# Gate and up projections as seven block products in place of eight, in a hand-ordered loop

## The chip, the cores and the metric

One core of a Trainium2 chip runs the whole layer in one launch. The metric is the device time in microseconds of that launch: 829.66 us is the median of 3 runs of the kernel before.

## What is computed

One decoder layer on 512 tokens with 1024 features: a mixer (dilated attention beside retention), a cross-attention to 256 memory rows, and a SwiGLU of 2816 hidden features, each between an RMSNorm of its input and an RMSNorm of its output, and added to the residual. The part that the change touches:

```python
def swiglu(h, w_gate_up, w_down):
    g, u = jnp.split(h @ w_gate_up, 2, axis=-1)
    return (jax.nn.silu(g) * u) @ w_down

for l in range(DEPTH):
    y = hybrid_mixer(rms_norm(x, pre_mix_g[l]), ...)
    x = x + rms_norm(y, post_mix_g[l])
    y = memory_cross_attn(rms_norm(x, pre_mem_g[l]), ...)
    x = x + rms_norm(y, post_mem_g[l])
    y = swiglu(rms_norm(x, pre_ffn_g[l]), w_gate_up[l], w_down[l])
    x = x + rms_norm(y, post_ffn_g[l])
```

## The kernel before, in words

The chip's engines are told of by their names in the trace: PE multiplies matrices, PEld loads its weights, DVE, ACT and POOL work element by element, SP issues most transfers. All data are fp32. Each factor of a product is kept as a high half (rounded to fp32r) and a low half (the rest), and `mm3` makes each product of three matmuls, high x high (L84), high x low (L85), low x high (L86). `split` makes the halves: ACT casts (L90), DVE subtracts (L91), so a weight block of 128x2048 costs ACT two casts and DVE two subtractions 1024 wide.

Weights come as transfers of 1 MB in a fixed order (`chunks`). `load` puts one into `raw` (two buffers) and splits it; `take` keeps one or two blocks ahead. So a fetch starts when the low half of the block two before it has freed the buffer.

The four blocks of 128 tokens end the memory attention one after another (`mem_block`, L780): 48 matmuls of the output projection, then `residual` (squares on ACT, the small per-token arithmetic of the reciprocal root on POOL, L137 to L141 and L625, the sums on DVE) and `normed` (the same again, then `h`, one DVE instruction 128x1024, L635). PE transposes `h` (L792) and `split` stores it feature by feature in `h3` (`to_h3`, L787). PE's order there: transposes of block 0, projection of block 2, transposes of block 1, projection of block 3, gate/up column block 0 for the first 256 tokens, transposes of block 2, column block 1 for the first 256 tokens, transposes of block 3, then both for the other 256.

The 22 column blocks of the gate/up product hold 128 gate and 128 up features each. From the third on (L834 to L838) one takes 2 x 8 x 3 = 48 matmuls of 512 columns (all tokens), gate into one PSUM bank and up into another; ACT takes the silu of the gate (L817), DVE multiplies by up (L820). `split_a` (L841) splits the result for the down projection, its low half on POOL (L846). The order of instructions on each engine is set by the framework's scheduler from the order of the code; the buffers decide what waits.

Of the kernel before, what the change touches and what calls it, by code (L numbers as in the profile page):

```python
# [11 lines left out]
F32 = mybir.dt.float32  # L12
# [7 lines left out]
P = 128  # L20
D = 1024
# [17 lines left out]
def hybrid_layer(ctx, tc, t, out):  # L39
# [20 lines left out]
    def pair(name):  # L60
        return unit(name + "h", F32R), unit(name + "l", F32R)
# [17 lines left out]
    def part(pr, c0, n):  # L79
        return pr[0][:, c0:c0 + n], pr[1][:, c0:c0 + n]  # L80
# [7 lines left out]
    def split(src, hi, lo, scale=None):  # L88
# [75 lines left out]

    def load_gain(name):
        g = wk.tile([P, D], F32, tag="g", name=uname("g"), bufs=2)
        src = t[name]
        nc.sync.dma_start(g, bass.AP(tensor=src.tensor, offset=src.offset, ap=[[0, P], [1, D]]))
        return g

# [7 lines left out]

# [1 line left out]
    gT = cp.tile([P, 3, KT], F32, name="gT")  # L180
# [70 lines left out]

# [1 line left out]
    def tok_proj(c0, name, evict):  # L253
# [48 lines left out]

# [1 line left out]
    off = [0, 512, 1024, 896]  # L304
# [62 lines left out]

# [1 line left out]
    qk = [unit("qk", F32R) for _ in range(4)]  # L369
# [50 lines left out]

# [1 line left out]
    scale = AD ** -0.5  # L422
# [86 lines left out]

# [1 line left out]
    mem = {}  # L511
# [74 lines left out]
    for i in range(AH):  # L586
# [12 lines left out]
        att_values(i)  # L599
# [176 lines left out]
    nat = tuple(range(KT))  # L776
    g4 = load_gain("pre_ffn_g")
    h3 = [pair("h3") for _ in range(2)]
# [26 lines left out]
    af = []  # L805

    def gx(k, c0, n):
        return part(h3[k // 4], (k % 4) * S + c0, n)

    def gate_up(w, pg, pu, c0, n):  # L810
        for j, ps in enumerate((pg, pu)):
            for k in range(KT):
                mm3(ps[:, c0:c0 + n], part(w, k * 256 + j * P, P), gx(k, c0, n), k == 0, k == KT - 1)

    def swish(f, pg, pu):
        sg = work("sg")
        nc.scalar.activation(sg, pg, AF.Silu)  # L817
# [93 lines left out]
def _layout(inp):  # L911
# [62 lines left out]
```

## Time and profile before

| What | Value |
|---|---|
| median of 3 runs | 829.66 us (829.64 to 830.22) |
| span of the profiled execution (the only time given of it) | 828.5 us |
| PE busy | 807.9 us, 98% |
| DVE busy | 396.6 us, 48% |
| ACT busy | 305.4 us, 37% |
| POOL busy | 132.8 us, 16% |

Busy times are sums of the intervals in which an engine worked on something; an engine with a low share can still be what another waits for at one place. The span stands in the same place as a run's time, without the little that lies around it.

### The profile page before, as it was taken

The page shows a single profiled execution, that of the slowest core. Times are in us where ns is not written, and L with a number is a line of the kernel's source. Part 1 is how long each engine was busy: PE and PEld are TensorE (multiplying, and loading weights), DVE is VectorE, ACT ScalarE, POOL GpSimd, SP SyncE. Part 2 cuts the span into 40 slices and gives each one's busy share as a digit, 9 for nine tenths or more (in the row PEclk, how much of TensorE's full clock was granted, in tenths as well). Part 3 has the DMA queues.
Part 4 walks back from the last instruction along what each step waited for, and adds up shares of the span by engine and source line. Part 5 has one row for each costly group of instructions (what it writes and reads, how often), then busy time and mean ns, then how long its engine had stood idle before and what let it go on. Part 6 is the DMA issues. An engine that isn't in the chain of part 4 may idle for free. (4 is left out here: it accounts for less than half of the span.)

```text
span 828.5 us, 10220 instructions
## 1 busy us (share of the span) xinstructions
PE 807.9 (98%) x4108; PEld 675.7 (82%) x4108; DVE 396.6 (48%) x766; ACT 305.4 (37%) x537; POOL 132.8 (16%) x176
## 2 busy tenths in 40 slices
PE   9979999999999999999999899999999999999996
PEld 7768888877777878999988788888888888888884
DVE  5595168764565657758446441405050314222144
ACT  5504333466464733445435232222130305332110
POOL 0161024410110100300036300000000004236000
PEclk9998999999999999999999999999999999999998
DMA  8726212221124440524002340505050322521011
GB/s 305 291 77 236 94 51 87 73 95 52 51 70 175 163 153 0 197 109 153 1 1 102 127 153 1 203 1 203 1 203 1 121 82 74 182 102 51 1 51 51
DMA packets 15519, 85.86 MB, mean 104 GB/s; under 512 B 1904, under 2 KB 1904, under 8 KB 6896
## 3 DMA queue, kind: packets, MB, share of 16 engines
q1 hardware_dynamic: 14752, 84.16, 27.7%
q10 hardware_dynamic: 720, 1.06, 0.3%
q8 instruction: 32, 0.52, 0.3%
q14 instruction: 15, 0.12, 0.0%
HBM read 83.11 MB, written 2.10 MB: 103 GB/s over the span
## 5 line engine op out<-in xcount | busy, mean ns | idle before, releaser
L91 DVE TENSOR_TENSOR wl<-raw,wh 128x1024 fp32r<-128x1024 f32 (+1 forms) x135 | 166.5, 1267 | 102.6 <-ACT wh L90 70.2
L90 ACT CAST wh<-raw 128x1024 fp32r<-128x1024 f32 (+1 forms) x135 | 133.8, 1042 | 95.3 <-DMA raw<-in_w_in 38.1
L820 DVE TENSOR_TENSOR af<-sg,u 128x512 f32<-128x512 f32 x22 | 15.1, 686 | 133.7 <-PE u L86 133.7
L846 POOL TENSOR_TENSOR al<-af,ah 128x512 fp32r<-128x512 f32 x22 | 34.6, 1605 | 257.5 <-ACT ah L845 243.3
L84 PE MATMUL g<-h3h,wh 128*128 128x512 f32 (+1 forms) x192 | 72.1, 375 | 0.0
L84 PE MATMUL u<-h3h,wh 128*128 128x512 f32 (+1 forms) x192 | 71.7, 373 | 0.0
L85 PE MATMUL g<-h3l,wh 128*128 128x512 f32 (+1 forms) x192 | 71.3, 371 | 0.0
L86 PE MATMUL g<-h3h,wl 128*128 128x512 f32 (+1 forms) x192 | 71.3, 371 | 0.0
L85 PE MATMUL u<-h3l,wh 128*128 128x512 f32 (+1 forms) x192 | 71.3, 371 | 0.0
L86 PE MATMUL u<-h3h,wl 128*128 128x512 f32 (+1 forms) x192 | 71.3, 371 | 0.0
L84 PE MATMUL dn<-wh,ah 128*128 128x512 f32 x176 | 68.5, 389 | 0.0
L85 PE MATMUL dn<-wl,ah 128*128 128x512 f32 x176 | 68.5, 389 | 0.0
L86 PE MATMUL dn<-wh,al 128*128 128x512 f32 x176 | 68.5, 389 | 0.0
L817 ACT ACTIVATE sg<-g 128x512 f32<-128x512 f32 x22 | 13.1, 598 | 149.2 <-PE g L86 123.0
L84 PEld LDWEIGHTS g<-h3h,wh 128*128 128x128 f32 x192 | 36.5, 190 | 6.5 <-ACT h3h L90 0.2
L84 PEld LDWEIGHTS u<-h3h,wh 128*128 128x128 f32 x192 | 36.6, 191 | 6.3
L85 PEld LDWEIGHTS g<-h3l,wh 128*128 128x128 f32 x192 | 36.2, 188 | 6.4
L86 PEld LDWEIGHTS g<-h3h,wl 128*128 128x128 f32 x192 | 36.2, 188 | 6.2
L85 PEld LDWEIGHTS u<-h3l,wh 128*128 128x128 f32 x192 | 36.2, 188 | 6.2
L86 PEld LDWEIGHTS u<-h3h,wl 128*128 128x128 f32 x192 | 36.1, 188 | 6.1
L84 PEld LDWEIGHTS dn<-wh,ah 128*128 128x128 f32 x176 | 33.0, 188 | 6.9
L86 PEld LDWEIGHTS dn<-wh,al 128*128 128x128 f32 x176 | 33.0, 188 | 6.9
(267 smaller groups left out, 1752.8 us busy)
## 6 DMA issues: line engine op xcount, KB each, us to landing
raw<-in_w_gu SPq DMA_DIRECT2D x22, 1024.0 KB, 4.8
raw<-in_w_in SPq DMA_DIRECT2D x12, 1024.0 KB, 5.1
raw<-in_w_dn SPq DMA_DIRECT2D x11, 1024.0 KB, 4.7
raw<-in_w_kv SPq DMA_DIRECT2D x8, 1024.0 KB, 4.7
x<-in_x SPq DMA_DIRECT2D x4, 1024.0 KB, 10.2
raw<-in_w_out SPq DMA_DIRECT2D x4, 1024.0 KB, 5.3
raw<-in_w_q SPq DMA_DIRECT2D x4, 1024.0 KB, 5.3
raw<-in_w_o SPq DMA_DIRECT2D x4, 1024.0 KB, 4.7
```

The source lines that it names most:

```text
L84: nc.tensor.matmul(o, lhsT=sh, rhs=mh, start=start, stop=False)
L85: nc.tensor.matmul(o, lhsT=sh, rhs=ml, start=False, stop=False)
L86: nc.tensor.matmul(o, lhsT=sl, rhs=mh, start=False, stop=stop)
L90: nc.scalar.copy(hi, src)
L91: nc.vector.tensor_sub(lo, src, hi.bitcast(F32))
L817: nc.scalar.activation(sg, pg, AF.Silu)
L820: nc.vector.tensor_mul(af[-1][:, (f % 4) * S:(f % 4 + 1) * S], sg, pu)
L846: nc.gpsimd.tensor_sub(lo[:, c], af[i][:, c], hi[:, c].bitcast(F32))
```

## The change

For the column blocks from the third on, the weights [gate over up] and the features are taken as 2 x 2 blocks (gate and up, first and last 512 features) and the tokens as two halves. In place of eight products of blocks seven are made, with sums of weight blocks (four per column block: s1, s3, s2, s4, on POOL) and sums of activation blocks (T1 to T4, made once), and the products are added to the results after. A product is 4 x 3 matmuls of 256 columns. Column blocks 0 and 1 keep eight products (`plain`).

- `blocks_sum` makes the four sums of 128x512 (L116 to L119) from `raw`; `blocks_split` splits 512 columns of `raw` (only the block that product 4 needs), the other 1024, and the two halves of the sums: 512 + 3 x 1024 in place of 2 x 1024.
- `step(f)` is the loop; `manual_schedule` keeps its order on every engine. Results: ACT copies a product out of PSUM (L879), DVE adds five times 256 columns and once 512, silu is in place on SBUF (L888), the product with up reads SBUF twice (L894).
- The small arithmetic of `mem_block` moves from POOL to DVE; the low halves of column blocks 0 and 1 move from DVE to POOL (L948).
- The tokens' `x` is written to DRAM ahead of the loop and read back behind it, to free room. Gains are loaded by pairs. `wk` has 6 buffers in place of 4.

```diff
-    def mem_block(b, mid=None):
-        residual(out_proj((b,), o_lhs, wo, nat, "o2", 0, mid)[b], b, g3, nc.gpsimd)
-        return normed(b, g4, nc.gpsimd)
+    def mem_block(b, mid=None):
+        e = nc.vector
+        residual(out_proj((b,), o_lhs, wo, nat, "o2", 0, mid)[b], b, g3, e)
+        return normed(b, g4, e)
...
+    def blocks_sum(f):
+        raw = blocks[f][0]
+        a11, a12, a22, a21 = (raw[:, i * 512:(i + 1) * 512] for i in range(4))
+        sums = rawp.tile([P, 2048], F32, tag="sums", name=uname("sums"))
+        s2, s4, s1, s3 = (sums[:, i * 512:(i + 1) * 512] for i in range(4))
+        nc.gpsimd.tensor_add(s1, a21, a22)
+        nc.gpsimd.tensor_sub(s3, a11, a21)
+        nc.gpsimd.tensor_sub(s2, s1, a11)
+        nc.gpsimd.tensor_sub(s4, a12, s2)
+        blocks[f] += [sums, pair("wa"), pair("wb")]
+
+    def blocks_split(f, i):
+        raw, sums, wa, wb = blocks[f]
+        src, w, c0, n = ((raw, wa, 1024, 512), (raw, wa, 0, 1024), (sums, wb, 1024, 1024), (sums, wb, 0, 1024))[i]
+        split(src[:, c0:c0 + n], *part(w, c0, n))
...
+    def to_b(h, b):
...
+        split(pv[0], *bview("B12", c0))
+        split(pv[1], *bview("B22", c0))
+        nc.vector.tensor_sub(t1, pv[0], braw[:, 0, :, c0:c0 + P])
+        nc.scalar.copy(b12, pv[0])
+        nc.vector.tensor_sub(t2, pv[1], t1)
+        nc.vector.tensor_sub(t3, pv[1], b12)
+        nc.gpsimd.tensor_sub(t4, braw[:, 1, :, c0:c0 + P], t2)
+        return lambda: [split(v, *bview(n, c0)) for v, n in ((t2, "T2"), (t1, "T1"), (t4, "T4"), (t3, "T3"))]
...
+    prods = {1: (0, 0, "B11"), 2: (0, 512, "B21"), 4: (0, 1024, "T4"), 5: (1, 1024, "T1"),
+             6: (1, 0, "T2"), 7: (1, 1536, "T3"), 3: (1, 512, "B22")}
+    def product(i, w, ps):
+        u, c0, name = prods[i]
+        for k in range(4):
+            x_ = bx[name][:, k * H:(k + 1) * H], bx[name][:, 1024 + k * H:1024 + (k + 1) * H]
+            mm3(ps, part(w[u], c0 + k * P, P), x_, k == 0, k == 3)
...
+    def ffn_c1(f):
+        nc.scalar.copy(s1[:, :H], p[:, :H])
+    def ffn_c11(f):
+        nc.vector.tensor_add(c[:, :H], s1[:, :H], p[:, H:])
+    def ffn_done(f):
+        nc.vector.tensor_add(c[:, H:], c[:, H:], r[:, H:])
+        nc.scalar.activation(c, c, AF.Silu)
+    def ffn_mult(f):
...
+        nc.vector.tensor_mul(af[-1][:, (f % 4) * S:(f % 4 + 1) * S], c, u)
+    def step(f):
+        nxt = f + 1 < FT
+        ffn_p12(f)
+        w, p, s1, c, u = ffn[f]
+        if f + 2 < FT:
+            blocks_sum(f + 2)
+        if f > PRE:
+            ffn_done(f - 1)
+        if nxt:
+            blocks_split(f + 1, 0)
+        ffn_c1(f)
+        if f > PRE:
+            ffn_mult(f - 1)
+        if nxt:
+            blocks_split(f + 1, 1)
+        if f + 3 < FT:
+            blocks_fetch(f + 3)
+        ffn_c11(f)
+        q, r = bank("q2"), bank("r")
+        ffn[f] += (r,)
+        product(4, w, q[:, :H])
+        product(6, w, r[:, :H])
+        if nxt:
+            blocks_split(f + 1, 2)
+        nc.vector.tensor_add(s1[:, H:], s1[:, :H], r[:, :H])
+        product(5, w, q[:, H:])
+        if nxt:
+            blocks_split(f + 1, 3)
+        nc.vector.tensor_add(c[:, H:], s1[:, H:], q[:, H:])
+        product(7, w, p[:, :H])
+        nc.vector.tensor_add(s1[:, :H], s1[:, H:], p[:, :H])
+        nc.vector.tensor_add(u.rearrange("p (i s) -> p i s", i=2), q.rearrange("p (i s) -> p i s", i=2),
+                             s1[:, None, :H].to_broadcast([P, 2, H]))
+        product(3, w, r[:, H:])
...
+    def plain_load(f):
+        blocks_fetch(f)
+        raw, w = blocks[f][0], pair("wa")
+        for i in range(4):
+            c = slice(i * 512, (i + 1) * 512)
+            nc.scalar.copy(w[0][:, c], raw[:, c])
+            nc.gpsimd.tensor_sub(w[1][:, c], raw[:, c], w[0][:, c].bitcast(F32))
...
-    for f in range(2, FT):
-        w, pg, pu = take("w_gu", f), bank("g"), bank("u")
-        gate_up(w, pg, pu, 0, S)
-        swish(f, pg, pu)
+    xd = tc.dram_tile([S, D], F32, name="xd")
+    for b in range(TB):
+        nc.sync.dma_start(xd[b * P:(b + 1) * P, :], x[b])
+    with tc.manual_schedule():
+        for f in range(PRE, FT):
+            step(f)
+        ffn_done(FT - 1)
+        ffn_mult(FT - 1)
+    bx.clear()
+    x = [unit("x") for _ in range(2)]
+    for i in range(2):
+        nc.sync.dma_start(x[i].rearrange("p (b d) -> p b d", b=2), xd[i * 256:(i + 1) * 256, :].rearrange("(b p) d -> p b d", p=P))
```

**DVE in the loop.** The rows of the kernel before from the last blocks, each line with its operands; `af` is the silu's product, `wl` a low half of weights:

```order
L820 TENSOR_TENSOR af_4862<-sg_4860,u_4811 128x512
L91 TENSOR_TENSOR wl_4866<-raw_4864,wh_4865 128x1024 x2
L91 TENSOR_TENSOR wl_4927<-raw_4925,wh_4926 128x1024 x2
L91 TENSOR_TENSOR wl_4988<-raw_4986,wh_4987 128x1024 x2
L820 TENSOR_TENSOR af_4862<-sg_4922,u_4873 128x512
```

And of the change, one step and the next step's first; `wal` and `wbl` are low halves of the weights and of their sums, `p`, `q`, `r` PSUM banks of products, `c` and `s` results in SBUF:

```order
L887 TENSOR_TENSOR c_5710<-c_5710,r_5733 128x256
L91 TENSOR_TENSOR wal_5718<-raw_5611,wah_5717 128x512
L894 TENSOR_TENSOR af_5844<-c_5710,u_5711 128x512
L91 TENSOR_TENSOR wal_5718<-raw_5611,wah_5717 128x1024
L883 TENSOR_TENSOR c_5828<-s_5827,p_5802 128x256
L91 TENSOR_TENSOR wbl_5720<-sums_5712,wbh_5719 128x1024
L920 TENSOR_TENSOR s_5827<-s_5827,r_5852 128x256
L91 TENSOR_TENSOR wbl_5720<-sums_5712,wbh_5719 128x1024
L924 TENSOR_TENSOR c_5828<-s_5827,q_5851 128x256
L926 TENSOR_TENSOR s_5827<-s_5827,p_5802 128x256
L927 TENSOR_TENSOR u_5829<-q_5851,s_5827 128x512
L887 TENSOR_TENSOR c_5828<-c_5828,r_5852 128x256
```

Three instructions per column block have become eleven, five of which read two tiles in SBUF. ACT's order in the same step of the change (`wah`, `wbh` are high halves, L888 is the silu):

```order
L888 ACTIVATE c_5710<-c_5710 128x512
L90 CAST wah_5717<-raw_5611 128x512
L879 COPY s_5827<-p_5802 128x256
L90 CAST wah_5717<-raw_5611 128x1024
L90 CAST wbh_5719<-sums_5712 128x1024 x2
```

The cast that DVE's second instruction needs stands behind the silu, which needs DVE's first.

**POOL ahead of the loop.** Before, it held the end of block 1's residual and its whole norm (`pr` and `nr` names, one element per token):

```order
L141 TENSOR_SCALAR pry_3929<-prw_3930,pry_3929 128x1
L155 TENSOR_SCALAR nrv_3945<-nrs_3942 128x1
L137 TENSOR_SCALAR nry_3947<-nrv_3945 128x1
L138 TENSOR_SCALAR nrn_3949<-nrv_3945 128x1
L140 TENSOR_SCALAR nrw_3948<-nry_3947,nrn_3949 128x1
L141 TENSOR_SCALAR nry_3947<-nrw_3948,nry_3947 128x1
```

Of the change, the same place; `sums_4343` and `sums_4485` are those of column blocks 2 and 3:

```order
L948 TENSOR_TENSOR wal_4180<-raw_4177,wah_4179 128x512 x4
L948 TENSOR_TENSOR wal_4192<-raw_4189,wah_4191 128x512 x4
L116 TENSOR_TENSOR sums_4343<-raw_4201 128x512
L117 TENSOR_TENSOR sums_4343<-raw_4201 128x512
L118 TENSOR_TENSOR sums_4343<-sums_4343,raw_4201 128x512
L119 TENSOR_TENSOR sums_4343<-raw_4201,sums_4343 128x512
L116 TENSOR_TENSOR sums_4485<-raw_4483 128x512
```

Block 1's chain now stands on DVE, between the residual's sums and `h`:

```order
L659 SCALAR_TENSOR_TENSOR x_2230<-z_3914,pry_3924,x_2230 128x512 x2
L181 TENSOR_SCALAR nrv_3940<-nrs_3937 128x1
L163 TENSOR_SCALAR nry_3942<-nrv_3940 128x1
L164 TENSOR_SCALAR nrn_3944<-nrv_3940 128x1
L166 TENSOR_SCALAR nrw_3943<-nry_3942,nrn_3944 128x1
L167 TENSOR_SCALAR nry_3942<-nrw_3943,nry_3942 128x1
```

Sixteen wide POOL instructions stand where the small ones did, and the small ones share DVE with the splits.

## Rows read from the trace of the kernel before

**Rows 1.** The page: the span, and busy time, share and instructions of each engine

```profile
span 828.5 us, 10220 instructions
PE 807.9 (98%) x4108; PEld 675.7 (82%) x4108; DVE 396.6 (48%) x766; ACT 305.4 (37%) x537; POOL 132.8 (16%) x176
```

**Rows 2.** Windows: us, busy (x count) of PE, PEld, DVE, ACT, POOL, clock, DMA, GB/s

```profile
465.00:473.00 8.00, 3.98 (x19) 3.58 (x19) 3.87 (x5) 2.84 (x4) 2.02 (x7) 0.79 0.00 0
483.00:700.00 217.00, 217.00 (x962) 179.85 (x962) 58.89 (x58) 50.91 (x62) 7.01 (x4) 1.00 0.27 97
```

**Rows 3.** Timeline, PE, 512-column matmuls, 17 intervals apart: start, us, engine, line, op, out<-in

```profile
490.25 0.39 PE L85 MATMUL u<-h3l,wh 128*128 128x512 f32 x1
...
494.11 0.39 PE L84 MATMUL g<-h3h,wh 128*128 128x512 f32 x1
```

**Rows 4.** Timeline, PE, 256-column matmuls 25 intervals apart, then the hole [idle <-releaser]

```profile
461.76 0.28 PE L85 MATMUL g<-h3l,wh 128*128 128x256 f32 x1
...
464.76 0.28 PE L86 MATMUL u<-h3h,wl 128*128 128x256 f32 x1
469.06 1.97 PE L792 MATMUL tp<-ident,h 128*128 128x128 f32 x8 [4.02 <-DVE h L635]
```

**Rows 5.** Timeline, DVE with POOL idle: the three shapes of the loop

```profile
397.51 2.13 DVE L91 TENSOR_TENSOR oTxl<-xo,oTxh 128x256 fp32r<-128x256 f32 x6
...
468.92 1.28 DVE L91 TENSOR_TENSOR h3l<-tp,h3h 128x512 fp32r<-128x512 f32 x2
...
516.74 4.62 DVE L91 TENSOR_TENSOR wl<-raw,wh 128x1024 fp32r<-128x1024 f32 x4
```

**Rows 6.** Timeline, ACT: a cast that waited for its weights; source view: silu and 512-wide casts

```profile
523.92 2.00 ACT L90 CAST wh<-raw 128x1024 fp32r<-128x1024 f32 x2 [1.76 <-DMA raw<-in_w_gu]
...
L817 ACT ACTIVATE sg<-g x22: 592/598/599, 475.6 to 698.6; 128x512 f32<-128x512 f32 x22
...
L845 ACT CAST ah<-af x22: 613/620/625, 689.9 to 757.1; 128x512 fp32r<-128x512 f32 x22
```

**Rows 7.** Source view, POOL's 128x512 subtraction: min/median/max ns

```profile
L846 POOL TENSOR_TENSOR al<-af,ah x22: 1283/1297/2284, 690.6 to 758.5; 128x512 fp32r<-128x512 f32 x22
```

**Rows 8.** Timeline, 690 us: POOL and DVE at work at once, 1024 wide

```profile
690.62 7.01 POOL L846 TENSOR_TENSOR al<-af,ah 128x512 fp32r<-128x512 f32 x4 [222.94 <-ACT ah L845]
690.82 4.42 DVE L91 TENSOR_TENSOR wl<-raw,wh 128x1024 fp32r<-128x1024 f32 x2
```

**Rows 9.** Timeline, 37 us: the same, 512 wide

```profile
37.53 7.82 POOL L242 TENSOR_TENSOR rope<-rope,rbc 128x512 f32<-128x512 f32 x4 [36.10 <-DVE rbc L177]
...
40.73 1.78 DVE L245 TENSOR_TENSOR t<-sc,rope 128x512 f32<-128x512 f32 x1
```

**Rows 10.** Timeline, 48 us: the same, one input of DVE in PSUM

```profile
48.06 0.69 DVE L245 TENSOR_TENSOR t<-rqk,rope 128x512 f32<-128x512 f32 x1
48.10 1.29 POOL L248 TENSOR_TENSOR rkT<-t,t 128x512 f32<-128x512 f32 x1 [0.83 <-DVE t L247]
```

**Rows 11.** Timeline, DVE's small instruction without POOL (110 us) and beside it (126 us)

```profile
110.17 0.17 DVE L143 TENSOR_SCALAR rry<-rvv 128x4 int32<-128x4 int32 x1
...
125.39 2.22 POOL L412 TENSOR_TENSOR t<-t,t 128x512 f32<-128x512 f32 x1
126.38 1.25 DVE L143 TENSOR_SCALAR rry<-rvv 128x4 int32<-128x4 int32 x1
```

**Rows 12.** Timeline and lines by form (count, us, mean ns, idle): block 1's chain, due times

```profile
430.46 1.07 ACT L90 CAST wh<-raw 128x1024 fp32r<-128x1024 f32 x1
...
439.30 1.29 DVE L635 SCALAR_TENSOR_TENSOR h<-x,nry,g 128x1024 f32<-128x1024 f32 x1 [3.08 <-POOL nry L141]
...
440.64 1.09 PE L792 MATMUL tp<-ident,h 128*128 128x128 f32 x8
...
L140 DVE TENSOR_SCALAR prw<-pry,prn 128x1 f32<-128x1 f32 x21 | 5.7, 272 | 0.7
```

**Rows 13.** The page's DMA issues: KB each, us from issue to landing

```profile
x<-in_x SPq DMA_DIRECT2D x4, 1024.0 KB, 10.2
```

More of the change, by code (lines that the diff above doesn't have):

```diff
@@ L99, in hybrid_layer, with blocks_fetch @@
     loaded = {}
+    blocks = {}
+    def blocks_fetch(f):
+        chunks.remove(("w_gu", f))
+        raw = rawp.tile([P, 2048], F32, tag="raw", name=uname("raw"))
+        nc.sync.dma_start(raw, t["w_gu"][f])
+        blocks[f] = [raw]
+    def blocks_sum(f):
[12 more added lines that the diff above has]
+        split(src[:, c0:c0 + n], *part(w, c0, n))
     def load(pieces=1, swap=False):
@@ L163, in load_rows, with load_gains @@
         return [x[b // 2][:, (b % 2) * D:(b % 2 + 1) * D] for b in range(TB)]
[L165 to L169, printed above, removed]
+    def load_gains(*names):
+        u = unit("g")
+        out = []
+        for i, name in enumerate(names):
+            src = t[name]
+            out.append(u[:, i * D:(i + 1) * D])
+            nc.sync.dma_start(out[-1], bass.AP(tensor=src.tensor, offset=src.offset, ap=[[0, P], [1, D]]))
+        return out
     def bcast_row(col, n, dst):
@@ L776, in hybrid_layer, with bview @@
     nat = tuple(range(KT))
-    g4 = load_gain("pre_ffn_g")
-    h3 = [pair("h3") for _ in range(2)]
-    def mem_block(b, mid=None):
-        residual(out_proj((b,), o_lhs, wo, nat, "o2", 0, mid)[b], b, g3, nc.gpsimd)
-        return normed(b, g4, nc.gpsimd)
-    def h3_block(h, b):
-        transposed(h, lambda half: [a.rearrange("p (k s) -> p k s", k=4) for a in h3[half]], S, b * P)
-    def to_h3(h, b):
+    bx, braw = {}, unit("braw").rearrange("p (i k s) -> p i k s", i=2, k=4)
+    def bview(name, c0):
+        if name not in bx:
+            bx[name] = unit("b" + name, F32R)
+        v = bx[name].rearrange("p (i k s) -> p i k s", i=2, k=4)
+        return v[:, 0, :, c0:c0 + P], v[:, 1, :, c0:c0 + P]
+    def mem_block(b, mid=None):
+        e = nc.vector
+        residual(out_proj((b,), o_lhs, wo, nat, "o2", 0, mid)[b], b, g3, e)
+        return normed(b, g4, e)
+    def to_b(h, b):
+        c0 = (b % 2) * P
+        pv = []
         for half in range(2):
@@ L792, in to_h3 @@
                 nc.tensor.transpose(ps[:, j * P:(j + 1) * P], h[:, k * P:(k + 1) * P], ident)
-            d = [a.rearrange("p (k s) -> p k s", k=4)[:, :, b * P:(b + 1) * P] for a in h3[half]]
-            split(ps.rearrange("p (k s) -> p k s", k=4), *d)
+            pv.append(ps.rearrange("p (k s) -> p k s", k=4))
+            if b < 2:
+                split(pv[half], *bview(("B11", "B21")[half], c0))
+                nc.scalar.copy(braw[:, half, :, c0:c0 + P], pv[half])
+        if b < 2:
+            return
+        tt = unit("t")
+        t1, t2, t3, t4 = (tt[:, i * 512:(i + 1) * 512].rearrange("p (k s) -> p k s", k=4) for i in range(4))
+        b12 = work("b12").rearrange("p (k s) -> p k s", k=4)
+        split(pv[0], *bview("B12", c0))
[6 more added lines that the diff above has]
+        return lambda: [split(v, *bview(n, c0)) for v, n in ((t2, "T2"), (t1, "T1"), (t4, "T4"), (t3, "T3"))]
     h = mem_block(0, lambda: x_transposes(3))
@@ L798, in hybrid_layer @@
     ha = mem_block(1)
-    to_h3(h, 0)
+    to_b(h, 0)
     hb = mem_block(2)
-    to_h3(ha, 1)
+    to_b(ha, 1)
     hc = mem_block(3)
     af = []
[L807 to L817, printed above, removed]
+    prods = {1: (0, 0, "B11"), 2: (0, 512, "B21"), 4: (0, 1024, "T4"), 5: (1, 1024, "T1"),
+             6: (1, 0, "T2"), 7: (1, 1536, "T3"), 3: (1, 512, "B22")}
@@ new lines, in hybrid_layer, with ffn_p12 @@
+    H = S // 2
+    def product(i, w, ps):
[3 more added lines that the diff above has]
+            mm3(ps, part(w[u], c0 + k * P, P), x_, k == 0, k == 3)
+    ffn = {}
+    def ffn_p12(f):
+        w, p = blocks[f][2:], bank("p")
+        product(1, w, p[:, :H])
+        product(2, w, p[:, H:])
+        ffn[f] = w, p, work("s1"), work("c"), work("u")
+    def ffn_c1(f):
+        w, p, s1, c, u = ffn[f]
+        nc.scalar.copy(s1[:, :H], p[:, :H])
@@ new lines, in hybrid_layer, with plain @@
+    PRE = 2
+    def plain(f, j, n, ps):
+        for i, (c0, name) in enumerate(((0, "B1%d"), (512, "B2%d")) if j == 0 else ((1536, "B1%d"), (1024, "B2%d"))):
+            v = bx[name % (n + 1)]
+            for k in range(4):
+                mm3(ps[:, n * H:(n + 1) * H], part(blocks[f], c0 + k * P, P),
+                    (v[:, k * H:(k + 1) * H], v[:, 1024 + k * H:1024 + (k + 1) * H]), i == k == 0, i == 1 and k == 3)
+    def plain_load(f):
[5 more added lines that the diff above has]
+            nc.gpsimd.tensor_sub(w[1][:, c], raw[:, c], w[0][:, c].bitcast(F32))
+        blocks[f] = w
@@ new lines, in hybrid_layer @@
+    pg = {f: (bank("g"), bank("u")) for f in range(PRE)}
+    plain_load(0)
+    plain_load(1)
+    blocks_fetch(2)
+    for f in range(PRE):
+        for j in range(2):
+            plain(f, j, 0, pg[f][j])
+        if f == 0:
+            late_splits = [to_b(hb, 2)]
+    late_splits.append(to_b(hc, 3))
+    blocks_sum(2)
+    for f in range(PRE):
+        for j in range(2):
+            plain(f, j, 1, pg[f][j])
+        if f == 0:
+            for e in late_splits:
+                e()
+            late_splits.clear()
+        del blocks[f]
+        sg = work("sg")
+        nc.scalar.activation(sg, pg[f][0], AF.Silu)
+        if f == 0:
+            af.append(unit("af"))
+        nc.vector.tensor_mul(af[0][:, f * S:(f + 1) * S], sg, pg[f][1])
+        for i in (2 * f, 2 * f + 1):
+            blocks_split(2, i)
@@ L839, in hybrid_layer @@
+    x = [x[b // 2][:, (b % 2) * D:(b % 2 + 1) * D] for b in range(TB)]
+    g5, = load_gains("post_ffn_g")
     aT = {}
@@ L940, in _layout @@
     gu = a["w_gate_up"][0]
-    w_gu = [tiles(gu, f * P, FF + f * P) for f in range(FT)]
+    w_gu = [blocks(gu, f * P, FF + f * P) for f in range(FT)]
     x = a["x"][0]
```

38 lines of the change are left out of this document (17 added, 21 removed).

## The prediction

> **What bounds the kernel now.** I read the page's busy times first, then windows of the stretch that is changed, then the timeline and the groups there. The page shows PE busy 807.9 of 828.5 us [rows 1], DVE half of it, ACT and POOL less: PE is the bound. That span belongs to the profiled execution; the median of the runs shown, 829.66 us, lies 1.2 us above it, and I carry that difference over.
>
> In the column-block loop the windows say it more sharply: in 217 us PE is busy for all 217 at full clock, DVE for 59, ACT for 51, POOL for 7 at the very end, and DMA for a quarter [rows 2]. So work taken from PE there is time won, until another engine needs more than PE per block. One matmul of 512 columns starts 3.86 / 17 = 0.2267 us after the one before it [rows 3]; 48 of them make 10.88 us per block, and 20 blocks 217.6 us.
>
> Just ahead of the loop PE has its one hole: 4.02 us before the last block's transposes, released by DVE's `h` [rows 4], with the clock at 0.79 over the 8 us around it, which is 0.21 x 8 = 1.7 us more [rows 2].
>
> **PE in the changed loop.** The seven products are 7 x 4 x 3 = 84 matmuls of 256 columns instead of 48 of 512. The columns fall by an eighth; the time does not, since a matmul of 256 columns takes 3.00 / 25 = 0.120 us [rows 4], more than half of 0.2267. A step is 84 x 0.120 = 10.08 us, against 10.88: 0.80 less, over 20 steps **-16.0 us** if PE stays the bound.
>
> **What a step asks of the others.** DVE gets five additions 256 wide (L883, L920, L924, L926, L887), one 512 wide (L927), the product c x u and a low half, 512 wide both, and three low halves 1024 wide. By the rows with POOL idle these take 2.13 / 6, less the overlap of neighbours, 0.34 each; 0.69 for L927 (a PSUM operand, [rows 10]); 0.60 for the 512s (1.28 / 2 less the overlap); 4.62 / 4 = 1.14 for the 1024s [rows 5]. The sum is 1.7 + 0.7 + 1.2 + 3.4 = 7.0 us. Before, it was one product and two low halves, 3.0.
>
> The written order adds a wait. After L887, DVE's next instruction is the 512-wide low half, and its cast stands on ACT behind the silu, which waits for L887: 0.60 + 0.62 = 1.2 us [rows 6] in which DVE stands with ready work queued behind. That gives 8.2 us for DVE, still under 10.08. ACT's five items (silu, cast 512, copy, three casts of 1.0) come to about 4.5 us, and POOL's four sums to 4 x 1.30 = 5.2 us [rows 7]. Each engine alone would fit under PE.
>
> **They are not alone.** Where POOL's 128x512 subtractions ran beside DVE's 1024-wide ones, two of DVE's took 4.42 us in place of 2.36 alone: 1.03 more each [rows 8]. The 512-wide one at 40.73 us took 1.78 instead of 0.69, 1.09 more [rows 9]. With one input in PSUM neither lost anything: 0.69 and 1.29 at the same moment [rows 10]. So DVE instructions with two SBUF inputs and POOL's take turns; in a step those are the two of 512 and the three of 1024.
>
> When do the four sums run? They need `raw`, which is fetched once the second low half has freed its buffer; in the rows a cast could follow 4.9 us after that (519.05, the end of the second of four low halves [rows 5], to 523.92 [rows 6]). By then DVE has come to its 1024-wide low halves of the sums; 5.2 us of POOL, stretched by the taking of turns, last until the low halves of the next step. I count three of the four as collisions: 3 x 1.03 = 3.1, so DVE needs 8.2 + 3.1 = **11.3 us per step**, more than PE's 10.08. None (POOL inside the wait and the PSUM additions) would leave 8.2, all four 12.3; stepping the queues by hand I get steps alternating between 10.6 and 11.9.
>
> The Trainium skill (SBUF — State Buffer, "SBUF: two separate sides") calls the port pair of DVE and GpSimd an exclusive lock, held for the whole instruction, that DVE takes with two SBUF inputs. The rows agree on who collides, but not on the price: 1.03, with 0.3 of overlap, not the full 1.30. By the rule taken strictly a step would come to 12.1 and the total some 11 us above mine.
>
> **The loop.** The second low half of the next block must stand when the next step begins. It is there about 4.4 us after a step's start, 5.6 ahead; falling behind by 1.2 per step uses that up in some four steps, which still take 10.08. The last two steps have no sums left to make. So 4 x 10.08 + 14 x 11.3 + 2 x 10.08 = 218.7, against 217.6: **+1 us**. Ends: 10.64 in each of the fourteen gives -8, 12.15 gives +13.
>
> **Ahead of the loop.** The small instructions of the four blocks' norms move from POOL to DVE, where such a one takes 0.27 us (the 21 at the end of the kernel, [rows 12]). POOL gets sixteen of 1.30 in their place: eight low halves of blocks 0 and 1, then the sums of blocks 2 and 3, some 21 us from about 432, since the first weights' cast starts at 430.46 [rows 12]. In that stretch lies the chain of token block 1: nine small instructions, then `h`, which ended at 440.6; PE came to its transposes at 440.64 without a wait [rows 12]. Does a small DVE instruction take turns with POOL? The nearest row says yes: one of 128x4, 0.17 alone, took 1.25 and ended with POOL's 2.22 [rows 11]. With eight of the chain's instructions held for a POOL one, 8 x 1.30 = 10.4: `h` at 451, and PE has an idle of some 10 us. The block 3 chain comes after POOL is done and is shorter by its cheaper instructions, so the old hole of 4 goes; a stretch at half clock is merely moved. Net **+6**. If 128x1 instructions do not take turns, the new hole is about 1.3 and the old one goes with its slow clock: -4, the lower end.
>
> **After the loop.** The last L887 and product, and the first low halves of the down weights, come later than PE's first six matmuls (6 x 0.2267 = 1.4 us) can cover: **+1** (0 to 3). The spill of x and its return ride on queues with three quarters free [rows 2]; x lands in some 10 us [rows 13], tens of us before the last residual; nothing. The gains come by pairs and earlier; nothing waits for them.
>
> **Sum.** +1 + 6 + 1 = +8: span 836.5, and with 1.2 around it **837.7 us**.
>
> **The rivals.** *A, small instructions do not take turns.* Loop as above, but -4 ahead of it: 829.7 + 1 - 4 + 1 = about 828. For it: an instruction of one element per partition has little to hold a port with, and the row that I lean on is 128x4; against it: that row is the only one. Price between 820 and 834 as the loop goes. The Trainium skill (VectorE: DVE Perf Modes, "What auto-detection actually checks") ties the two-port mode of a one-source instruction to its outermost non-unit dimensions, and 128x1 has none, so the rule leaves this open; no run here shows a 128x1 beside POOL.
>
> *B, PE stays the bound.* If POOL's sums fall mostly into DVE's wait and its additions from PSUM, fewer than two collisions are left (8.2 + 1.9 = 10.1 is the point from which it decides), and the loop gives its full -16. With +6 and +1: 820.7; with the small instructions free as well, 810.7. For it: 1.2 us of wait and 2.4 us of PSUM additions per step are room for three sums. Against: the sums start when `raw` lands, which is tied to DVE's own low half and puts them beside the next ones.
>
> *C, the worst phase.* All four sums collide in each step, 12.15, and the stops cost clock as the hole did: +13 + 6 + 1, 849.7. For it: a delayed low half delays the fetch and so the next sums, so the phase may lock; against: the alternation that I get by hand breaks it.
>
> *D, the change does not do what it says:* 84 matmuls and four sums per step stand in the program's order, so I give it nothing.
>
> **How the numbers follow.** Forecast 0.42 (slower; with the lower end of its loop, 837.7 - 9 = 829; with a loop between it and C's, up to some 845); A 0.18 (0.06 faster, 0.06 within, 0.06 slower); B 0.30 (faster); C 0.10 (slower). About 0.2%, 1.7 us, is what a measurement of this kernel can tell from no change. Faster 0.06 + 0.30 = 0.36, same 0.06, slower 0.42 + 0.06 + 0.10 = 0.58. The forecast and C alone run from 829 to 850. The range reaches down through most of B and leaves out its lowest part, and up past C: 812 to 851.
>
> **What would show it.** In the profile after: intervals of 0.120 between matmuls inside a product; steps of 11 to 12 us in the middle of the loop with PE idle ahead of a step's first product, released by DVE's low half (L91); 1024-wide low halves near 2.2 us and POOL's sums above 1.30; the first steps at 10.08 and the last two as well. Ahead of the loop: PE idle some 10 us before block 1's transposes, released by `h`, and small DVE instructions near 1.3 us. I am wrong if steps stay at 10.1 (then the sums do not collide where I put them), or if the small instructions beside POOL stay at 0.27.

## The result and the profile after

The changed kernel takes 833.37 us (median of 5 runs, 832.77 to 835.61), the kernel before 829.80 (5 runs): a ratio of 1.0046, with an interval of 1.0034 to 1.0059. It is slower by 3.6 us, where 8 were forecast. Two terms of the sum were off by 10 and by 8 us in opposite directions; that the whole came out as near as it did is luck. The profiled execution of the change is the slowest of its five (835.61). Of all executions in this document one, of run 2, took 1568.9 us where its other three took 809.5 to 810.7, and its ratio leaves it out.

The page of the profiled execution after, its span and its busy times, answers to [rows 1]:

```profile
span 833.8 us, 12068 instructions
PE 797.6 (96%) x4828; PEld 698.0 (84%) x4828; DVE 553.2 (66%) x1012; ACT 351.0 (42%) x615; POOL 245.8 (29%) x190
```

PE has 10.3 us less work than before, DVE 157 us more, POOL 113 us more. The stretch from 483 to 700 us, as in [rows 2] (us, busy of PE, PEld, DVE, ACT, POOL, clock, DMA share, GB/s):

```profile
483.00:700.00 217.00, 198.51 (x1605) 193.73 (x1605) 189.58 (x209) 83.11 (x116) 116.40 (x73) 1.00 0.29 102
```

PE was busy for all of it before; now it stands for 18.5 us, at full clock. What PE waits for in the whole execution, the three lines that matter here (us in total, times, longest):

```profile
PE p L84 <- DVE c L883: 14.3, 17, 1.6
...
PE r L84 <- DVE s L920: 4.2, 9, 0.5
...
PE tp L827 <- DVE h L664: 0.9, 1, 0.9
```

Two of them are waits in the middle of a step, before product 7 (tile `p`) and product 3 (tile `r`). The third is what is left of the hole of 4.02 us [rows 4]: 0.9.

For the difference stage by stage one needs the borders of the loop. Before (PE's timeline): the first 512-column matmul of column block 2 and the first of the down projection.

```profile
483.65 0.40 PE L85 MATMUL g<-h3l,wh 128*128 128x512 f32 x1
...
700.83 0.39 PE L84 MATMUL dn<-wh,ah 128*128 128x512 f32 x1
```

After (the same): product 1 of column block 2, and the down projection's first six matmuls of high by high halves.

```profile
479.24 0.28 PE L84 MATMUL p<-bB,wah 128*128 128x256 f32 x1
...
705.41 1.55 PE L84 MATMUL dn<-wh,ah 128*128 128x512 f32 x6
```

| Stretch | before | after | difference | forecast |
|---|---|---|---|---|
| start to loop | 483.65 | 479.24 | -4.4 | +6 |
| loop | 217.2 | 226.2 | +9.0 | +1 |
| behind it, to the span's end | 127.7 | 128.4 | +0.7 | +1 |

The differences of the profiled executions sum to 5.3 us, their spans' difference (833.8 - 828.5); the medians differ by 3.6. Runs 1, 3 and 6 to 8 below have the change's code ahead of the loop, and in their profiles the loop starts at 477.5 to 479.1: the -4.4 is the small end of what that stretch gains.

**The step of the loop.** DVE's groups from 500 to 680 us by form (count, busy us, mean ns, idle before):

```profile
L91 DVE TENSOR_TENSOR wbl<-sums,wbh 128x1024 fp32r<-128x1024 f32 x32 | 45.5, 1423 | 0.0
L91 DVE TENSOR_TENSOR wal<-raw,wah 128x1024 fp32r<-128x1024 f32 x16 | 37.1, 2317 | 0.0
L894 DVE TENSOR_TENSOR af<-c,u 128x512 f32<-128x512 f32 x16 | 28.6, 1786 | 0.0
L91 DVE TENSOR_TENSOR wal<-raw,wah 128x512 fp32r<-128x512 f32 x16 | 19.9, 1244 | 19.7 <-ACT wah L90 19.7
...
L883 DVE TENSOR_TENSOR c<-s,p 128x256 f32<-128x256 f32 x15 | 6.1, 408 | 0.0
```

Beside an idle POOL such instructions take 1.22 (1024 wide) and 0.69 (512 wide), as run 8 below has them. Against that the two low halves of the sums lose 0.20 each, that of `raw` 1.10, the product 1.10, the 512-wide low half 0.55: 3.2 us per step. These losses are called turns from here on. L883, with an operand in PSUM, stays at 0.41 for itself, 0.34 behind a neighbour. And the wait behind silu and cast is there, 19.7 us in 16 steps: 1.2. One step shows who meets whom; first DVE, then POOL:

```profile
605.32 0.41 DVE L887 TENSOR_TENSOR c<-c,r 128x256 f32<-128x256 f32 x1
606.94 1.03 DVE L91 TENSOR_TENSOR wal<-raw,wah 128x512 fp32r<-128x512 f32 x1 [1.21 <-ACT wah L90]
607.89 1.78 DVE L894 TENSOR_TENSOR af<-c,u 128x512 f32<-128x512 f32 x1
609.59 2.32 DVE L91 TENSOR_TENSOR wal<-raw,wah 128x1024 fp32r<-128x1024 f32 x1
611.83 0.41 DVE L883 TENSOR_TENSOR c<-s,p 128x256 f32<-128x256 f32 x1
```

```profile
606.13 1.29 POOL L116 TENSOR_TENSOR sums<-raw 128x512 f32<-128x512 f32 x1 [6.13 <-DMA raw<-in_w_gu]
607.38 1.75 POOL L117 TENSOR_TENSOR sums<-raw 128x512 f32<-128x512 f32 x1
609.09 1.74 POOL L118 TENSOR_TENSOR sums<-sums,raw 128x512 f32<-128x512 f32 x1
610.91 2.14 POOL L119 TENSOR_TENSOR sums<-raw,sums 128x512 f32<-128x512 f32 x1
```

The sums start at 606.13 when `raw` lands, go through the wait of 1.21 us, and then each of DVE's next three instructions ends 0.5 to 1.1 us after one of POOL's does, in line with its own time alone. Over 15 steps, from one L927 to another, the mean step is (673.98 - 502.22) / 15 = 11.45 us:

```profile
502.22 0.69 DVE L927 TENSOR_TENSOR u<-q,s 128x512 f32<-128x512 f32 x1
...
673.98 0.69 DVE L927 TENSOR_TENSOR u<-q,s 128x512 f32<-128x512 f32 x1
```

**The start of the loop.** DVE's L883 in the first two steps, and PE's first matmul of product 7 in the same steps:

```profile
484.81 0.41 DVE L883 TENSOR_TENSOR c<-s,p 128x256 f32<-128x256 f32 x1
...
497.77 0.41 DVE L883 TENSOR_TENSOR c<-s,p 128x256 f32<-128x256 f32 x1
```

```profile
486.44 0.28 PE L84 MATMUL p<-bT,wbh 128*128 128x256 f32 x1
...
498.32 0.36 PE L84 MATMUL p<-bT,wbh 128*128 128x256 f32 x1 [1.65 <-DVE c L883]
```

In the first step L883 is done 1.2 us ahead of product 7 (485.22 to 486.44). DVE's next cycle takes 12.96 us, and product 7 of the second step already waits 1.65 us for it. That cycle is longer than the mean because POOL makes the sums of two column blocks in it, eight instructions one right behind the other:

```profile
484.94 1.30 POOL L116 TENSOR_TENSOR sums<-raw 128x512 f32<-128x512 f32 x1 [13.03 <-DVE wal L91]
...
496.84 2.14 POOL L119 TENSOR_TENSOR sums<-raw,sums 128x512 f32<-128x512 f32 x1
```

So all five of DVE's wide instructions meet one: the low halves of the sums take 2.17 and 1.98 us, the 512-wide low half 1.43, the product 1.78, the 1024-wide low half of `raw` 2.31. Their turns are 4.6 us in place of 3.2, and the cycle is 1.5 longer than 11.45. From one first matmul of product 1 to the next, PE's steps are 10.08, 12.66, 11.50, 11.58, then 14 of 11.44 in the mean, and two of 10.08.

**Ahead of the loop.** POOL's eight low halves, two small DVE instructions and `h` of token block 1 in the middle of them, and PE's transposes of that block:

```profile
433.54 11.94 POOL L948 TENSOR_TENSOR wal<-raw,wah 128x512 fp32r<-128x512 f32 x8 [80.60 <-ACT wah L947]
...
438.82 0.27 DVE L166 TENSOR_SCALAR nrw<-nry,nrn 128x1 f32<-128x1 f32 x1
439.13 0.21 DVE L167 TENSOR_SCALAR nry<-nrw,nry 128x1 f32<-128x1 f32 x1
...
440.50 1.33 DVE L664 SCALAR_TENSOR_TENSOR h<-x,nry,g 128x1024 f32<-128x1024 f32 x1
...
441.88 0.33 PE L827 MATMUL tp<-ident,h 128*128 128x128 f32 x1 [0.91 <-DVE h L664]
```

The small instructions take 0.27 and 0.21 us beside a busy POOL. `h` ends at 441.8, 1.2 later than before [rows 12], and PE idles 0.91 us instead of the 10 that were forecast. What the chain lost it lost in wide instructions: the two sums of the residual (L659, 128x512) take 3.20 us beside POOL, where the two took 1.42 before (L630). The old hole with its half clock does not come back; the 8 us around it, as in [rows 2]:

```profile
465.00:473.00 8.00, 7.76 (x64) 7.33 (x62) 6.60 (x11) 5.84 (x11) 2.79 (x2) 1.00 0.00 0
```

### The profile page after: what moved, and what is told of

Its sections match the earlier page's. It is cut to its first block, busy times and chain, and to the rows that moved or that the text cites. A ratio compares the mean times of both kernels' runs of the same rounds, so it can differ in the third digit from the quotient of the medians.

```text
span 833.8 us, 12068 instructions
## 1 busy us (share of the span) xinstructions
PE 797.6 (96%) x4828; PEld 698.0 (84%) x4828; DVE 553.2 (66%) x1012; ACT 351.0 (42%) x615; POOL 245.8 (29%) x190
## 4 chain that ended last, share of the span: by engine, by line
PE 53%; DVE 29%; issue 8%; ACT 5%; POOL 3%; DMA 2%; DVEq 0%; SPq 0%; ACTq 0%; POOLq 0%
DVE wal L91 7%; PE dn L85 5%; PE dn L86 5%; PE dn L84 5%; DVE af L894 3%; DVE wl L91 3%; DVE wbl L91 3%; PE o L85 2%; PE o L86 2%; PE o L84 2%; PE oT L507 2%; DMA raw<-in_w_out 1%; PE q L85 1%; PE q L86 1%; PE q L84 1%
## 5 line engine op out<-in xcount | busy, mean ns | idle before, releaser
L91 DVE TENSOR_TENSOR wl<-raw,wh 128x1024 fp32r<-128x1024 f32 (+1 forms) x91 | 112.9, 1273 | 69.0 <-ACT wh L90 45.2
L90 ACT CAST wh<-raw 128x1024 fp32r<-128x1024 f32 (+1 forms) x91 | 90.3, 1039 | 73.0 <-DMA raw<-in_w_in 36.6
L91 DVE TENSOR_TENSOR wal<-raw,wah 128x512 fp32r<-128x512 f32 (+1 forms) x40 | 66.4, 1661 | 24.7 <-ACT wah L90 24.7
L888 ACT ACTIVATE c<-c 128x512 f32<-128x512 f32 x20 | 12.6, 632 | 124.6 <-DVE c L887 124.6
L91 DVE TENSOR_TENSOR wbl<-sums,wbh 128x1024 fp32r<-128x1024 f32 x40 | 57.0, 1425 | 0.0
L116 POOL TENSOR_TENSOR sums<-raw 128x512 f32<-128x512 f32 x20 | 25.9, 1294 | 91.6 <-DMA raw<-in_w_gu 66.6
L84 PE MATMUL p<-bB,wah 128*128 128x256 f32 x160 | 45.3, 283 | 0.0
L85 PE MATMUL p<-bB,wah 128*128 128x256 f32 x160 | 45.3, 283 | 0.0
L86 PE MATMUL p<-bB,wal 128*128 128x256 f32 x160 | 45.3, 283 | 0.0
L90 ACT CAST wbh<-sums 128x1024 fp32r<-128x1024 f32 x40 | 39.9, 1049 | 0.0
L119 POOL TENSOR_TENSOR sums<-raw,sums 128x512 f32<-128x512 f32 x20 | 36.2, 1810 | 1.6
L85 PE MATMUL q<-hhl,wh 128*128 128x256 f32 x128 | 36.2, 284 | 0.2 <-DVE hhl L91 0.2
L86 PE MATMUL q<-hhh,wl 128*128 128x256 f32 x128 | 36.1, 283 | 0.0
```

The lines of the kernel that those rows point to most:

```text
L84: nc.tensor.matmul(o, lhsT=sh, rhs=mh, start=start, stop=False)
L85: nc.tensor.matmul(o, lhsT=sh, rhs=ml, start=False, stop=False)
L86: nc.tensor.matmul(o, lhsT=sl, rhs=mh, start=False, stop=stop)
L90: nc.scalar.copy(hi, src)
L91: nc.vector.tensor_sub(lo, src, hi.bitcast(F32))
L116: nc.gpsimd.tensor_add(s1, a21, a22)
```

## Experiments

All times are medians; ratios are to the kernel before, run on the same chip.

**1. Banks of their own for products 7 and 3.**

```diff
-        q, r = bank("q2"), bank("r")
-        ffn[f] += (r,)
+        q, r, m, n = bank("q2"), bank("r"), bank("m"), bank("n")
+        ffn[f] += (n,)
...
-        product(7, w, p[:, :H])
-        nc.vector.tensor_add(s1[:, :H], s1[:, H:], p[:, :H])
+        product(7, w, m[:, :H])
+        nc.vector.tensor_add(s1[:, :H], s1[:, H:], m[:, :H])
...
-        product(3, w, r[:, H:])
+        product(3, w, n[:, H:])
```

> Products 7 and 3 get PSUM banks of their own, so that PE no longer waits in the middle of a step for DVE's L883 and L920, which read the other half of the same bank. Nothing is left out. Theory 1 (DVE's cycle of 11.4 us per step, made of its work, the turns that it takes with POOL and 1.2 us behind silu and cast, sets the pace; the two waits only decide how much of DVE's first delay PE can ignore): the waits come back as a wait for the low half ahead of product 1 or 2, steps in the middle stay near 11.4, and only the start's slack grows from 1.2 to about 4.6 us, so 3 to 4 us less than the 833.4 of the change: about 830. Rival (the waits on shared banks tie PE and DVE into a circle that sets the pace): steps fall towards 10.1 and the loop by up to 24 us: about 812.

Measured: 830.55 us, ratio 1.0003 (0.9992 to 1.0014), 2.8 less than the change by medians and 3.6 by the ratios. The waits of PE:

```profile
PE p L86 <- DVE wal L91: 16.2, 15, 1.7
```

The waits in the middle of a step are gone, and the same time is spent ahead of product 1 or 2, waiting for the low half. The mean of 15 of DVE's cycles is 11.44, as before the edit. DVE's cycle sets the pace; the shared banks cost the slack at the start and no more. PE's first four steps now take 10.08 each, as forecast, in place of 10.08, 12.66, 11.50 and 11.58, and the loop of the profiled execution lasts 221.6 us in place of 226.2.

**2. Sums made once.**

```diff
-        if f + 2 < FT:
-            blocks_sum(f + 2)
+        if f + 2 < FT:
+            blocks[f + 2] += [sums0[0], pair("wa"), pair("wb")]
```

> The sums of column block 2 are used for all later blocks, so the four POOL instructions of each step are left out (the sums of the other blocks are not computed); DVE, ACT and PE keep every instruction. Theory 1 (turns between POOL and DVE): DVE's step falls to its own work of 7.0 to 7.6 us and the wait of 1.2, under PE's 10.08, so PE stays busy through the loop: 20 x 10.08 = 201.6 in place of 226.2, and the whole about 809. Rival (DVE's own instructions and the wait behind silu and cast are too much without any collision, the sums are innocent): steps stay over 11 us and the time over 828.

Measured: 810.66 us, ratio 0.9763 (0.9747 to 0.9779), close to the 809 of theory 1. The same stretch of the loop:

```profile
483.00:700.00 217.00, 216.74 (x1727) 212.85 (x1726) 152.43 (x225) 95.76 (x132) 11.74 (x8) 1.00 0.35 124
```

PE is busy for all of it but the step to the down projection, with DVE's instructions unchanged in number (1012 in the whole kernel) and the wait behind silu and cast still there (20.9 us in 17 steps). Without POOL in the loop every step takes 10.08. The loop was lost to POOL's sums, not to DVE's own share of the work; that it is by the turns, and not by something else that the sums bring, is for runs 7 and 8 to show.

**3. The 512-wide cast ahead of the silu.**

```diff
+        if nxt:
+            blocks_cast0(f + 1)
         if f > PRE:
             ffn_done(f - 1)
         if nxt:
-            blocks_split(f + 1, 0)
+            blocks_low0(f + 1)
```

(`blocks_cast0` is the cast of `blocks_split(f + 1, 0)` alone, `blocks_low0` its subtraction.)

> On ACT the 512-wide cast of the next block's weights is written ahead of the silu; DVE's order stays. Nothing is left out. Theory 1: the 1.2 us in which DVE stands behind add, silu and cast are part of its 11.4 us cycle, so a step falls by about 1.2 to 10.1 or 10.3, close to PE's own: loop 203 to 208, the whole 811 to 816. Rival (DVE stands there while POOL makes a sum anyway, so that a collision takes the place of the wait): steps stay between 11.0 and 11.4, the whole 826 to 833.

Measured: 820.71 us, ratio 0.9888 (0.9873 to 0.9903): between the two. The mean step is 10.6, a gain of 0.85 of the 1.2. DVE's groups from 500 to 680 us:

```profile
L91 DVE TENSOR_TENSOR wbl<-sums,wbh 128x1024 fp32r<-128x1024 f32 x35 | 58.6, 1674 | 0.0
L91 DVE TENSOR_TENSOR wal<-raw,wah 128x1024 fp32r<-128x1024 f32 x17 | 32.5, 1911 | 7.1 <-ACT wah L90 6.6
L902 DVE TENSOR_TENSOR af<-c,u 128x512 f32<-128x512 f32 x17 | 26.8, 1579 | 1.1 <-ACT c L896 0.9
L133 DVE TENSOR_TENSOR wal<-raw,wah 128x512 fp32r<-128x512 f32 x17 | 18.1, 1064 | 0.0
```

The 512-wide low half no longer waits. The 1024-wide low half of `raw` now waits for its own cast, 0.4 us per step, and the low halves of the sums have become dearer, 1.67 in place of 1.42: POOL's sums are moved to other neighbours. By the same count as above the turns cost 2 x 0.46 + 0.70 + 0.89 + 0.38 = 2.9 us per step, after 3.2.

**4. The kernel before, with the pieces ahead of the loop.** The norms' small instructions on DVE, the low halves of column blocks 0 and 1 on POOL, everything else as before.

```diff
-        residual(out_proj((b,), o_lhs, wo, nat, "o2", 0, mid)[b], b, g3, nc.gpsimd)
-        return normed(b, g4, nc.gpsimd)
+        residual(out_proj((b,), o_lhs, wo, nat, "o2", 0, mid)[b], b, g3, nc.vector)
+        return normed(b, g4, nc.vector)
...
+        if key in (("w_gu", 0), ("w_gu", 1)):
+            for i in range(4):
+                c = slice(i * 512, (i + 1) * 512)
+                nc.scalar.copy(w[0][:, c], raw[:, c])
+                nc.gpsimd.tensor_sub(w[1][:, c], raw[:, c], w[0][:, c].bitcast(F32))
+            loaded[key] = w
+            return
```

> The kernel before, with two pieces of the change that lie ahead of the loop: the small instructions of the four norms on DVE, the low halves of column blocks 0 and 1 on POOL. Nothing is left out. Theory 1 (these alone close the hole of 4.0 us and spare the half clock behind it, and small DVE instructions do not take turns with POOL): 4 to 5 us less than before, 825. Rival (the hole closes because the transposes and the loop's first weights come in another order in the change): the hole stays or moves, 829 to 832.

Measured: 824.30 us, ratio 0.9933 (0.9916 to 0.9949). The hole ahead of the transposes shrinks to

```profile
PE tp L799 <- DVE h L642: 0.2, 1, 0.2
```

from 4.02. The loop starts at 477.52 in place of 483.65 and lasts 217.2 us as before, so the whole gain lies ahead of it. The two pieces together are worth 5.5 to 6 us; the profile of the change has 4.4, with 0.9 us of new hole. They were not taken apart.

**5. The norms back on POOL in the change.**

```diff
     def mem_block(b, mid=None):
-        e = nc.vector
+        e = nc.gpsimd
```

> The change with the small instructions of the four norms back on POOL; the loop is untouched and nothing is left out. Theory 1 (ahead of the loop POOL is full with wide instructions for some 21 us, and the small ones, in line between them, each wait for what stands ahead): the chain of block 2 or 3 is late, a hole of 4 us or more comes back ahead of its transposes, 4 to 10 us more than the 833.4 of the change. Rival (the gain of 4.4 us ahead of the loop comes from the low halves that DVE no longer makes there): 832 to 834.

Measured: 850.43 us, ratio 1.0242 (1.0225 to 1.0258): 17 us more than the change, where 4 to 10 were expected. POOL's timeline in the chain of block 2:

```profile
449.43 1.29 POOL L116 TENSOR_TENSOR sums<-raw 128x512 f32<-128x512 f32 x1
450.70 0.27 POOL L654 TENSOR_SCALAR pv<-ps,pv 128x1 f32<-128x1 f32 x1
450.92 1.30 POOL L117 TENSOR_TENSOR sums<-raw 128x512 f32<-128x512 f32 x1
```

The small instructions stand in line behind wide ones, here the first of them. PE's wait for `h`:

```profile
PE tp L827 <- DVE h L664: 13.2, 3, 8.6
```

Three holes of 13.2 us in all in place of one of 0.9, 12.3 more; the longest, 8.6, ends in transposes at half clock (1.97 us for the eight, as in [rows 4], against 1.04 to 1.09 elsewhere; the granted clock from 468 to 470 us is 0.50, the level of 1.2 GHz). By the profiles the loop starts 15.3 us later than in the change. The direction was right, the size not: I had counted one hole.

**6. Both casts first, and own banks.** As runs 1 and 3, and the 1024-wide cast of `raw` also ahead of the silu.

```diff
+        if nxt:
+            blocks_cast(f + 1, 1024, 512)
+            blocks_cast(f + 1, 0, 1024)
         if f > PRE:
             ffn_done(f - 1)
         if nxt:
-            blocks_split(f + 1, 0)
+            blocks_low(f + 1, 1024, 512)
         ffn_c1(f)
         if f > PRE:
             ffn_mult(f - 1)
         if nxt:
-            blocks_split(f + 1, 1)
+            blocks_low(f + 1, 0, 1024)
```

> Both casts of the next block's weights ahead of the silu on ACT, and products 7 and 3 in banks of their own. Nothing is left out. Theory 1 (a step is DVE's own 7.3 us, what it waits for ACT, and three or four turns with POOL at about 1.0): DVE no longer waits for ACT, steps fall to 10.1 to 10.5, the loop to 202 to 210, the whole 810 to 817. Rival (POOL takes each moment that DVE gives, so that a step stays at the 10.6 of the run with one cast first): 820.

Measured: 815.67 us, ratio 0.9828 (0.9812 to 0.9845). The whole lies where theory 1 had it, the step does not: 10.6, as in run 3 and as the rival said. DVE's groups:

```profile
L91 DVE TENSOR_TENSOR wbl<-sums,wbh 128x1024 fp32r<-128x1024 f32 x34 | 55.0, 1618 | 0.0
L133 DVE TENSOR_TENSOR wal<-raw,wah 128x1024 fp32r<-128x1024 f32 x17 | 38.4, 2256 | 0.0
L902 DVE TENSOR_TENSOR af<-c,u 128x512 f32<-128x512 f32 x18 | 27.6, 1533 | 1.3 <-ACT c L896 1.2
L133 DVE TENSOR_TENSOR wal<-raw,wah 128x512 fp32r<-128x512 f32 x17 | 22.0, 1296 | 0.0
```

Of the waits for ACT 1.3 us in 18 steps are left, and the turns have gone up to 2 x 0.40 + 1.04 + 0.84 + 0.61 = 3.3 us: POOL took what the casts gave. The 5 us against run 3 do not come from a shorter cycle but from the room that DVE has to lag: with a cycle of 10.6 the lag grows by half a microsecond per step, PE's first eight steps take 10.08, and its wait for the low half is down to the row below. How much of that room comes from the banks and how much from the casts was not taken apart.

```profile
PE p L86 <- DVE wal L133: 2.7, 6, 0.5
```

**7. The sums on DVE.** As run 6, with the four sums behind L927 on DVE, so that POOL rests in the loop.

```diff
-    def blocks_sum(f):
+    def blocks_sum(f, e=None):
+        e = e or nc.gpsimd
...
-        nc.gpsimd.tensor_add(s1, a21, a22)
+        e.tensor_add(s1, a21, a22)
...
-        if f + 2 < FT:
-            blocks_sum(f + 2)
...
                              s1[:, None, :H].to_broadcast([P, 2, H]))
+        if f + 2 < FT:
+            blocks_sum(f + 2, nc.vector)
```

> As the run before this one, and the four sums of a step are made by DVE behind L927, so that POOL does nothing in the loop. Nothing is left out. Theory 1 (the turns cost more than the sums): DVE needs 7.3 + 4 x 0.60 = 9.7 us per step and meets nobody, under 10.08: PE stays busy, loop 202 to 204, the whole 808 to 812. Rival (the order puts the sums ahead of L887, on whose result silu and the next product wait, and DVE at 97% has no room): steps over 10.5, 818 or more.

Measured: 810.09 us, ratio 0.9759 (0.9744 to 0.9774). The stretch of the loop, and two of DVE's groups:

```profile
483.00:700.00 217.00, 216.74 (x1731) 213.01 (x1730) 193.85 (x295) 93.25 (x131) 11.51 (x8) 0.95 0.35 124
```

```profile
L134 DVE TENSOR_TENSOR wal<-raw,wah 128x1024 fp32r<-128x1024 f32 x17 | 20.7, 1218 | 0.0
L903 DVE TENSOR_TENSOR af<-c,u 128x512 f32<-128x512 f32 x18 | 12.5, 693 | 2.7 <-ACT c L897 1.6
```

With the four sums added to DVE, PE is as busy as in run 2, which had left them out, and every step takes 10.08. The column of the clock reads 0.95 over this whole execution, while 84 matmuls still take 10.08 us; the other three executions read 0.99 and take 809.6 to 810.2 us, so I draw nothing from it. This version computes all and is faster than both kernels: 19.7 us under the one before.

**8. The sums on DVE alone.** The sums are moved as in run 7; casts and banks are as in the change.

> The change with its four sums made by DVE behind L927 and nothing else altered: casts and banks as in the change. Nothing is left out. Theory 1: the turns, 3.0 us per step by the rows, go, and 4 x 0.60 = 2.4 us of work come; the 1.2 us behind silu and cast stay: 11.4 - 3.0 + 2.4 = 10.8 per step, the loop about 216 in place of 226, the whole 822 to 826. Rival (the wait behind silu and cast vanishes with POOL's collisions, so casts and banks were not needed): 808 to 812, as with them. Second rival (the turns are not the cost, DVE is only given more to do): 860 or more.

Measured: 824.58 us, ratio 0.9937 (0.9918 to 0.9956), in the band of theory 1. The mean step over 15 is 10.85. Two of DVE's groups and PE's wait:

```profile
L91 DVE TENSOR_TENSOR wal<-raw,wah 128x1024 fp32r<-128x1024 f32 x17 | 20.8, 1225 | 0.0
L91 DVE TENSOR_TENSOR wal<-raw,wah 128x512 fp32r<-128x512 f32 x17 | 11.8, 693 | 20.9 <-ACT wah L90 20.9
```

```profile
PE p L84 <- DVE c L884: 9.1, 17, 0.6
```

The 1024-wide low half is back at 1.22, the 512-wide at 0.69, and the 1.2 us behind silu and cast are still there, 20.9 us in 17 steps. Moving 5.2 us of POOL work onto DVE as 2.4 us saved 0.6 us per step (11.45 - 10.85); by the count of the turns, 3.2 - 2.4, it would be 0.8.

## Why the prediction was wrong in its size

The direction, the bound and the price of a step came out; two terms did not.

- **PE's share**: 84 matmuls in 10.08 us, shown by runs 2 and 7 to a hundredth, against 10.88. (3.86 / 17 is 0.2271 and not 0.2267; the loop before took 217.2 us for the 217.6 of the sum.) The -16 us were there to be had: run 2's loop has them.
- **The step at 11.3 us**: measured 11.45 (15 steps). Own work of 7 us, 1.2 of wait, and turns of 3.1 by forecast, 3.2 by the rows. (The range was drawn less carefully: four collisions are 12.3 in one place and 12.15 in another, and 10.64 has no working.) That the size of the turns held is in part luck, since I had put them in the wrong place: I expected them at the low halves of the sums, and they fell on the product and the two low halves of `raw`. My own figures said so. If `raw` lands 4.9 us after the 1024-wide low half that frees its buffer (5.05 in the step shown above, 601.08 to 606.13), DVE is by then through both low halves of the sums, the additions and L887, 4.7 us by the prices in the prediction. Runs 7 and 8 show that the turns are the cost.
- **The loop's start, failed: +9 in place of +1.** "It is there about 4.4 us after a step's start, 5.6 ahead", hence "some four steps, which still take 10.08". I looked only at the low half that product 1 of the next step needs. Product 7 writes into the bank whose other half L883 reads, and L883 stands behind that same low half on DVE: the slack was 1.2 us, by the timelines of L883 and product 7. DVE's first cycle of 12.96 used it up at once, so one step and not four took 10.08: 12.66, 11.50 and 11.58 for the next three are 5.5 us too many, and 0.14 more than forecast in each of the 14 later steps is 2. Run 1, with banks of their own, has the four steps at 10.08.
- **Ahead of the loop, failed: -4.4 in place of +6.** "Does a small DVE instruction take turns with POOL? The nearest row says yes." It does not: 0.14 to 0.28 us each beside POOL's wide ones. The row that I leaned on is of 128x4 elements, the chain's are of 128x1. The term is the -4 of rival A, and run 4 has it alone. The Trainium skill (VectorE: DVE Perf Modes, "What auto-detection actually checks") makes the two-port mode of a one-source instruction hang on its outermost non-unit dimension. The 128x4 that was held fits that; 128x1 has no such dimension, so the rule does not say that it goes free, and no run varied the shape by itself.
- **Behind the loop**: +0.7 for +1.
- **The lock.** The Trainium skill (SBUF — State Buffer, "SBUF: two separate sides") has DVE and GpSimd take the shared port pair for a whole instruction. Who meets whom agrees with it in every group of the loop above: instructions with two inputs in SBUF lose time, those with one in PSUM do not. A single meeting costs up to 1.1 us of POOL's 1.30; per step the four sums of 5.2 us cost DVE 2.9 to 3.3 in each of the three orders tried.

So the likeliest case of the forecast was a mixture: its loop was worse than its centre, and its ends were those of rival A. Rival B needed fewer than two turns a step and had the price of three. What remains open: whether the sums on POOL could be placed beside DVE's additions from PSUM alone, which was not tried.

## What to carry to other kernels

Work moved to an idle engine is not free when that engine shares a path with the one that sets the pace: count the meetings, and compare their sum with the work itself; here four sums cost less on the busy engine (2.4 us) than on the idle one (3.2 us of turns). Freeing a wait of the loaded engine does not shorten a cycle by that wait, if another engine was using the time. And a slack must be counted to the nearest wait of the same bank, not to the next step's operand.

## What was not expected of the hardware

Small DVE instructions of 128x1 run at their own speed (0.14 to 0.28 us) beside POOL instructions of 128x512, while one of 128x4 was held for over 1 us [rows 11]. The other way round POOL's wide subtractions were stretched too: eight took 11.94 us in place of 10.4 beside DVE's work ahead of the loop. And the turns' total per step hardly depended on the order of the instructions: 3.2, 2.9 and 3.3 us in the change and runs 3 and 6.
